# One early small read of x beside the first loads, and the last 256 output columns as one tile, two copies and one store

## The chip, the cores and the metric

The kernel runs on one core of a Trainium2 chip. The metric is the device time in microseconds (us) of that core, taken as the median of several runs; less is better. The profile of one run has a "span" that is about 1.8 us shorter than the time of the same run. Each kernel has one profile, of one execution.

## The reference

```python
def reference(x, gamma, w_qkv, eps):        # x: 8 x 1024 x 768, w_qkv: 768 x 2304, float32
    rms = np.sqrt(np.mean(x ** 2, axis=-1, keepdims=True) + eps)
    x_norm = x / rms * gamma
    return np.matmul(x_norm, w_qkv).astype(np.float32)
```

It is a matrix product of 8192 rows with 768 x 2304 weights, with a scale per row. The kernel folds gamma into the weights (converted to bf16) and applies 1/rms when it copies the product out of PSUM.

## The kernel before

Rows are worked in 64 tiles of 128. For the first six (the head) a fixed plan says in which order small loads, transposes and matmuls come; the rest is a steady loop. Loads and stores are issued by the sync engine (SP), gamma by ScalarE.

```python
LOADS = [  # order of issue on SP: "w" is a chunk of weights, "x" a tile of 128 rows (384 KB)
    (-9.00, "w", 0), (-8.99, "x", 0), (-8.98, "x", 1), (-8.97, "x", 2), (-8.96, "w", 1),
    (-8.95, "w", 2), (-8.94, "w", 3), (-8.93, "x", 3), (-8.92, "w", 4), ...
]
PARTS = [(0, 1024), (1024, 1024), (2048, N - 2048)]        # column ranges of an output row; the last is 256 wide
...
    g6 = singles.tile([KO, P], f32)
    nc.scalar.dma_start(out=g6, in_=gamma.rearrange("(ko p) -> ko p", p=P))
    eps_sb = singles.tile([P, 1], f32)
    nc.vector.memset(eps_sb, float(eps))
    tbl = singles.tile([P, 1], f32)
    nc.scalar.activation(out=tbl, in_=eps_sb, func=AF.Sqrt)      # loads ScalarE's table early
...
    def width(t, n0):                                            # columns of one PSUM tile
        return P if t == MT - 1 and n0 >= N - 2 * P else min(NT, N - n0)

    def evac(t, n0, eng):                                        # PSUM -> SBUF, times 1/rms
        nl = width(t, n0)
        ...
        if eng == "DVE":
            nc.vector.tensor_scalar(out=o, in0=pm[:, :nl], scalar1=RS[t], scalar2=None, op0=mult)
        else:
            nc.scalar.activation(out=o, in_=pm[:, :nl], func=AF.Copy, scale=RS[t], bias=0.0)
...
    def evac_at(time, t, n0, eng, gap):
        at(time, evac, t, n0, eng)
        h = part(n0)
        nl = width(t, n0)
        left[t, h] = left.get((t, h), PARTS[h][1]) - nl
        if t >= MT - 2:                                          # last two tiles: a store per copy
            at(time + gap - 0.5, store, t, h, n0, nl)
        elif left[t, h] == 0:
            at(time + gap, store, t, h, *PARTS[h])
...
        for n0 in [*range(0, N, NT)] + [N - P] * (t == MT - 1):  # last tile: 4 x 512, 128, 128 columns
            at(now, mm, t, n0, range(KO))
            now += width(t, n0) * US
            flip ^= 1
            evac_at(now + 0.2, t, n0, "DVE" if flip else "ACT", gap=1.2)
```

So the very end of the kernel is: a 512-wide PSUM tile copied by VectorE and stored (256 KB), then two 128-wide PSUM tiles, one copied by ScalarE and one by VectorE, each with its own store of 64 KB.

Of the kernel before, what the change touches and what calls it, by code (L numbers as in the profile page):

```python
# [10 lines left out]
HEAD = 6  # L11
# [81 lines left out]
def kernel(  # L93
# [8 lines left out]
    nc = tc.nc  # L102
    f32 = mybir.dt.float32
    bf16 = mybir.dt.bfloat16
    AF = mybir.ActivationFunctionType
    mult = mybir.AluOpType.mult

    xf = x.flatten_outer_dims()
    of = out.flatten_outer_dims()
    M, K = xf.shape  # L110
    Kw, N = w_qkv.shape
    assert K == Kw
    P = 128
    KO = K // P
    MT = M // P
    NT = 512
# [6 lines left out]
    singles = ctx.enter_context(tc.tile_pool(name="singles", bufs=1))  # L123
# [11 lines left out]
    ones = nc.const_aps.tensor(1.0, [P, NT], bf16)  # L135
    g6 = singles.tile([KO, P], f32)
    nc.scalar.dma_start(out=g6, in_=gamma.rearrange("(ko p) -> ko p", p=P))
    eps_sb = singles.tile([P, 1], f32)
    nc.vector.memset(eps_sb, float(eps))

# [10 lines left out]
    X, XB, XT, RS, OUT, WF, PM, PT = {}, {}, {}, {}, {}, {}, {}, {}  # L151
# [71 lines left out]
    begun = {}  # L223

    def width(t, n0):

        return P if t == MT - 1 and n0 >= N - 2 * P else min(NT, N - n0)

    def mm(t, n0, kos):
        nl = width(t, n0)  # L230
        for ko in kos:
            if (t, n0) not in PM:
                PM[t, n0] = psum.tile([P, NT], f32, name="pm")
            b = begun[t, n0] = begun.get((t, n0), 0) + 1
            nc.tensor.matmul(out=PM[t, n0][:, :nl], lhsT=XT[t][:, ko, :], rhs=w_b[:, ko, n0:n0 + nl],  # L235
                             start=(b == 1), stop=(b == KO))

    def part(n0):
        return max(i for i, (p0, _) in enumerate(PARTS) if p0 <= n0)

    def evac(t, n0, eng):
        nl = width(t, n0)
        h = part(n0)
        if (t, h) not in OUT:
            OUT[t, h] = outp.tile([P, PARTS[h][1]], f32, name=f"ot{h}")
        o = OUT[t, h][:, n0 - PARTS[h][0]:n0 - PARTS[h][0] + nl]
        pm = PM[t, n0]
        if eng == "DVE":
            nc.vector.tensor_scalar(out=o, in0=pm[:, :nl], scalar1=RS[t], scalar2=None, op0=mult)  # L249
        else:  # L250
            nc.scalar.activation(out=o, in_=pm[:, :nl], func=AF.Copy, scale=RS[t], bias=0.0)  # L251

    def store(t, h, n0, nl):
        p0 = PARTS[h][0]
# [6 lines left out]
    def at(time, fn, *args):  # L261
        plan.append((time, len(plan), fn, args))
# [8 lines left out]
# [5 lines that stand above are left out]
        if t >= MT - 2:  # L276
# [3 lines that stand above are left out]
# [27 lines left out]
    for t in range(HEAD, MT):  # L307

        ahead = 6.0 if t < HEAD + 5 else 0.0
        if ("x", t) not in {q[1:] for q in LOADS}:  # L310
            at(now - 15 - ahead, load_x, t)
        at(now - 8.5 - ahead, cast, t)
        at(now - 7.5 - ahead, xbar, t)
        at(now - 5, stat, t)
        at(now - 3, recip, t)
        for n0 in [*range(0, N, NT)] + [N - P] * (t == MT - 1):
            at(now, mm, t, n0, range(KO))
            now += width(t, n0) * US
            flip ^= 1
            evac_at(now + 0.2, t, n0, "DVE" if flip else "ACT", gap=1.2)  # L320
# [38 lines left out]
```

## Time and profile before

| | before |
|---|---|
| time, median of 3 runs | 388.26 us (388.1 to 388.3) |
| time in the runs beside the changed kernel, 6 runs | 388.21 us (387.88 to 388.62) |
| time and span of the profiled run | 388.64 us, 386.857 us |
| first main matmul | 8.09 us |
| span end, counted from the start of the last 512-wide copy | 4.292 us |

The page and the two ends are shown in the prediction below. ScalarE's timeline at the start (start, duration, engine, line, operation): the issue of the gamma load, then the table load.

```profile
0.73 0.58 ACTq L137 DMA_DIRECT2D g<-in_gamma_dram  x1
1.35 1.28 ACT L142 ACT_TABLE_LOAD   x1 [1.35 <-PEq L340]
```

A stretch of the chain of work that ended last:

```profile
16.13 6.01 DMA x_t<-in_x_dram
...
22.75 6.20 DMA xT<-xb
28.95 0.05 issue
```

After the head, x is transposed by a DMA (xT<-xb). At 28.95 us the chain passes from such a DMA to TensorE.

### The profile page before, as it was taken

How to read it: one execution, taken by the hardware profiler on the slowest of the kernel's cores; microseconds unless marked ns; L12 is line 12 of the kernel's file. 1: busy time of each engine (PE TensorE's matmuls, PEld its weight loads, DVE VectorE, ACT ScalarE, POOL GpSimd, SP SyncE). 2: the span in 40 equal slices, each digit the busy share in tenths (PEclk: the TensorE clock that was granted, in tenths of full speed). 3: DMA queues.
4: the chain of work that ended last, by engine and by line, in shares of the span. 5: the costliest groups of instructions: out<-in, count | busy, mean ns of one | idle time of the engine just before them, and what ended most of it. 6: DMA issues, size and time to landing. Idle time of an engine off the chain costs nothing.

```text
span 386.9 us, 5470 instructions
## 1 busy us (share of the span) xinstructions
PE 379.9 (98%) x1927; PEld 192.2 (50%) x1965; DVE 153.4 (40%) x307; ACT 181.6 (47%) x365; POOL 6.5 (2%) x14
## 2 busy tenths in 40 slices
PE   8999999999999999999999999999999999999996
PEld 4444655454554554554554554554554554554553
DVE  2744534434333344333344333343333343333332
ACT  4752644453544443544444444544444534434532
POOL 0130000000000000000000000000000000000000
PEclk9999999999999999999999999999999999999999
DMA  8999999999999999999999999999999999999985
GB/s 291 390 281 402 398 318 363 344 338 283 351 297 308 303 295 321 293 300 322 305 289 313 285 318 312 293 309 275 326 311 297 304 317 305 304 306 289 292 264 186
DMA packets 89719, 119.91 MB, mean 310 GB/s; under 512 B 52438, under 2 KB 61532, under 8 KB 89692
## 3 DMA queue, kind: packets, MB, share of 16 engines
q1 hardware_dynamic: 89680, 119.56, 101.2%
q8 instruction: 15, 0.25, 0.3%
q14 instruction: 12, 0.10, 0.1%
q10 hardware_dynamic: 12, 0.00, 0.0%
HBM read 32.25 MB, written 75.50 MB: 279 GB/s over the span
## 4 chain that ended last, share of the span: by engine, by line
PE 89%; DMA 8%; issue 1%; DVE 1%; ACT 1%; SPq 0%
PE pm L235 89%; DMA x_t<-in_x_dram 3%; DMA w_f<-in_w_qkv_dram 2%; DMA xT<-xb 2%; DMA out_dram<-ot 1%; ACT ot L251 1%; DVE ot L249 0%; DVE xb L174 0%; SPq L160 0%; SPq L155 0%; SPq L255 0%; ACT w_b L168 0%
## 5 line engine op out<-in xcount | busy, mean ns | idle before, releaser
L235 PE MATMUL pm<-w_b,xT 128*128 128x512 bf16 (+1 forms) x1888 | 372.1, 357 | 2.1
L235 PEld LDWEIGHTS <-xT 128*128 128x128 bf16 x1926 | 187.9, 98 | 185.5 <-DMA xT<-xb 0.5
L249 DVE TENSOR_SCALAR ot<-pm,rstd 128x512 f32<-128x512 f32 (+1 forms) x161 | 111.5, 695 | 206.1 <-PE pm L235 201.7
L251 ACT ACTIVATE ot<-pm,rstd 128x512 f32<-128x512 f32 (+2 forms) x160 | 102.7, 643 | 191.7 <-PE pm L235 151.0
L185 ACT ACTIVATE sq<-x_t 128x768 bf16<-128x768 f32 x64 | 53.4, 834 | 3.0 <-DMA x_t<-in_x_dram 3.0
L174 DVE CAST xb<-x_t 128x768 bf16<-128x768 f32 x61 | 33.2, 545 | 13.6 <-DMA x_t<-in_x_dram 13.5
L187 ACT ACTIVATE rms<-ssq,eps_sb 128x1 f32<-128x1 f32 x64 | 18.8, 294 | 2.1
L185 ACT ACTIVATION_READ_ACCUMULATOR sq<-x_t 128x1 f32 x64 | 12.2, 191 | 0.0
L166 DVE TENSOR_SCALAR w_b<-w_f,g_sb 128x512 bf16<-128x512 f32 (+1 forms) x16 | 7.7, 499 | 5.9 <-DMA w_f<-in_w_qkv_dram 5.9
L192 DVE RECIPROCAL rstd<-rms 128x1 f32<-128x1 f32 x64 | 9.8, 153 | 0.0
L170 POOL TENSOR_SCALAR w_b<-w_f,g_sb 128x512 bf16<-128x512 f32 (+1 forms) x8 | 5.8, 735 | 23.5 <-DMA w_f<-in_w_qkv_dram 23.5
L284 PE MATMUL pm<-const-bfloat16-1.0 128*128 128x512 bf16 (+1 forms) x14 | 5.4, 539 | 0.8 <-PEq L340 0.8
L168 ACT ACTIVATE w_b<-w_f,g_sb 128x512 bf16<-128x512 f32 (+1 forms) x6 | 3.6, 612 | 2.7 <-DMA w_f<-in_w_qkv_dram 2.7
L212 PE MATMUL pm<-ident_f,x_t 128*128 128x128 f32 x18 | 2.8, 300 | 0.3 <-DMA x_t<-in_x_dram 0.3
L212 PEld LDWEIGHTS pm<-ident_f,x_t 128*128 128x128 f32 x18 | 2.4, 160 | 1.3 <-DMA x_t<-in_x_dram 0.9
L284 PEld LDWEIGHTS <-const-bfloat16-1.0 128*128 128x128 bf16 x14 | 1.5, 126 | 2.7 <-issue 2.7
L176 ACT CAST xT<-pm 128x256 bf16<-128x256 f32 (+1 forms) x5 | 2.3, 458 | 0.9 <-PE pm L212 0.7
L142 ACT ACT_TABLE_LOAD x1 | 1.3, 1283 | 1.4 <-PEq L340 1.4
L174 DVE CAST xT<-pm 128x512 bf16<-128x512 f32 x1 | 0.7, 691 | 1.4 <-PE pm L212 1.4
L267 DVE COPY g_sb<-pm 128x6 f32<-128x6 f32 x1 | 0.2, 164 | 1.9 <-PE pm L266 1.9
L266 PEld LDWEIGHTS pm<-ident_f,g 6*128 6x128 f32 x1 | 0.2, 177 | 1.0 <-issue 1.0
L174 DVE COPY xT<-pm 128x768 bf16<-128x768 bf16 x1 | 0.6, 557 | 0.0
(12 smaller groups left out, 2.5 us busy)
## 6 DMA issues: line engine op xcount, KB each, us to landing
out_dram<-ot SPq DMA_DIRECT2D x124, 512.0 KB, 3.9
x_t<-in_x_dram SPq DMA_DIRECT2D x64, 384.0 KB, 4.2
out_dram<-ot SPq DMA_DIRECT2D x63, 128.0 KB, 3.2
w_f<-in_w_qkv_dram SPq DMA_DIRECT2D x10, 512.0 KB, 7.4
out_dram<-ot SPq DMA_DIRECT2D x8, 256.0 KB, 2.0
w_f<-in_w_qkv_dram SPq DMA_DIRECT2D x4, 256.0 KB, 6.6
xT<-xb SPq DMA_TRANSPOSE x60, 4.3
w_f<-in_w_qkv_dram SPq DMA_DIRECT2D x2, 384.0 KB, 6.1
```

What stands on the lines that cost most here:

```text
L166: nc.vector.tensor_scalar(out=o, in0=i, scalar1=g, scalar2=None, op0=mult)
L168: nc.scalar.activation(out=o, in_=i, func=AF.Copy, scale=g, bias=0.0)
L170: nc.gpsimd.tensor_scalar(out=o, in0=i, scalar1=g, scalar2=1.0, op0=mult, op1=mult)
L174: nc.vector.tensor_copy(out=out, in_=in_)
L185: nc.scalar.activation(out=sq, in_=X[t], func=AF.Square, accum_out=ssq)
L187: nc.scalar.activation(out=rms, in_=ssq, func=AF.Sqrt, scale=inv_k, bias=eps_sb)
L192: nc.vector.reciprocal(out=r, in_=RS[t])
L212: nc.tensor.transpose(out=PT[t, h][:, ko - k0, :], in_=X[t][:, ko * P:(ko + 1) * P], identity=ident_f)
L235: nc.tensor.matmul(out=PM[t, n0][:, :nl], lhsT=XT[t][:, ko, :], rhs=w_b[:, ko, n0:n0 + nl], start=(b == 1), stop=(b == KO))
L249: nc.vector.tensor_scalar(out=o, in0=pm[:, :nl], scalar1=RS[t], scalar2=None, op0=mult)
L251: nc.scalar.activation(out=o, in_=pm[:, :nl], func=AF.Copy, scale=RS[t], bias=0.0)
L284: nc.tensor.matmul(out=wps[:, :nl], lhsT=ones[:, :P], rhs=ones[:, :nl], start=True, stop=True)
```

## The change

The first part adds a small DMA on ScalarE: 16 floats of every sixteenth row of the head's 768 rows, 48 pieces of 64 bytes, into a tile that nobody uses. What it can be meant for is the loads of x that come after it. The second part ends the last row tile with one 256-column PSUM tile: VectorE copies its first half, ScalarE its second, and one 128 KB store takes the place of two of 64 KB.

```diff
     nc.scalar.dma_start(out=g6, in_=gamma.rearrange("(ko p) -> ko p", p=P))
+    touch = singles.tile([HEAD * P // 16, 16], f32)
+    nc.scalar.dma_start(out=touch, in_=xf[:HEAD * P].rearrange("(r s) k -> r s k", s=16)[:, 0, :16])
...
     def width(t, n0):
-        return P if t == MT - 1 and n0 >= N - 2 * P else min(NT, N - n0)
+        return min(NT, N - n0)
...
-        if eng == "DVE":
-            nc.vector.tensor_scalar(out=o, in0=pm[:, :nl], scalar1=RS[t], scalar2=None, op0=mult)
-        else:
-            nc.scalar.activation(out=o, in_=pm[:, :nl], func=AF.Copy, scale=RS[t], bias=0.0)
+        both = t == MT - 1 and n0 + nl == N
+        d = nl if eng == "DVE" and not both else P if both else 0
+        if d:
+            nc.vector.tensor_scalar(out=o[:, :d], in0=pm[:, :d], scalar1=RS[t], scalar2=None, op0=mult)
+        if d < nl:
+            nc.scalar.activation(out=o[:, d:], in_=pm[:, d:nl], func=AF.Copy, scale=RS[t], bias=0.0)
...
-        for n0 in [*range(0, N, NT)] + [N - P] * (t == MT - 1):
+        for n0 in range(0, N, NT):
```

## The prediction

> **What bounds the kernel now.** I read the page first, then the chain of work that ended last, then the timelines of the two ends, because the change touches nothing in between.
>
> ```profile
> span 386.9 us, 5470 instructions
> PE 379.9 (98%) x1927; PEld 192.2 (50%) x1965; DVE 153.4 (40%) x307; ACT 181.6 (47%) x365; POOL 6.5 (2%) x14
> ...
> L235 PE MATMUL pm<-w_b,xT 128*128 128x512 bf16 (+1 forms) x1888 | 372.1, 357 | 2.1
> ```
>
> TensorE is the bound: its main matmuls are 372.1 us busy in a span of 386.9 us, and it idled only 2.1 us ahead of them. The span is 1.4 us shorter than the time of 388.26 us; I take that offset as constant. So the change can only win in the two places where TensorE isn't streaming: the start, before about 8.1 us, and the tail, after the last matmul at about 383.2 us.
>
> The start, from the chain in order of time, TensorE's timeline, and the table by windows (its columns: stretch, length, busy us of each engine, clock, DMA share, GB/s):
>
> ```profile
> 1.75 5.58 DMA x_t<-in_x_dram
> 7.33 0.02 issue
> 7.35 7.38 DMA w_f<-in_w_qkv_dram
> ...
> 28.99 6.00 PE pm L235 x27
> ```
>
> ```profile
> 5.91 1.14 PE L212 MATMUL pm<-ident_f,x_t 128*128 128x128 f32 x6
> 7.38 0.88 PE L212 MATMUL pm<-ident_f,x_t 128*128 128x128 f32 x6 [0.32 <-DMA x_t<-in_x_dram]
> 8.09 0.59 PE L235 MATMUL pm<-w_b,xT 128*128 128x512 bf16 x2
> ```
>
> ```profile
> 1.00:2.00 1.00, 1.00 (x3) 0.29 (x2) 0.23 (x1) 0.65 (x1) 0.29 (x1) 1.00 0.34 25
> 2.00:3.00 1.00, 1.00 (x3) 0.15 (x1) 0.00 (x0) 0.84 (x2) 0.00 (x0) 1.00 0.64 197
> 3.00:4.00 1.00, 0.86 (x4) 0.46 (x4) 0.16 (x1) 0.00 (x0) 0.00 (x0) 1.00 1.04 389
> 4.00:5.00 1.00, 1.00 (x3) 0.30 (x2) 0.38 (x1) 0.00 (x0) 0.00 (x0) 1.00 1.08 405
> 5.00:6.00 1.00, 1.00 (x4) 0.43 (x3) 0.51 (x2) 0.50 (x1) 0.00 (x0) 1.00 1.05 366
> 6.00:7.00 1.00, 1.00 (x7) 0.82 (x5) 0.12 (x1) 0.73 (x3) 0.00 (x0) 1.00 0.95 367
> ```
>
> The reader is to see three things. The chain leaves through the load of the second tile of x (issued 1.75, landed 7.33 us). TensorE, which must transpose that tile next, idles 0.32 us for it. And the DMA engines are busy in 1-3 us while moving little (share 0.34 at 25 GB/s, 0.64 at 197 GB/s), and again move a little less in 5-7 us (366 against 405 GB/s): some early packets are slow. The first x tile landed at 5.48 us (ScalarE starts on it at 5.50), so the second came 1.85 us later, while 384 KB at the 405 GB/s seen beside it take 0.97 us. About 0.88 us was lost there (estimate from these figures).
>
> The tail, from three timelines of short windows and the DMA view:
>
> ```profile
> 382.56 1.02 DVE L249 TENSOR_SCALAR ot<-pm,rstd 128x512 f32<-128x512 f32 x2 [1.84 <-DMA out_dram<-ot]
> 382.90 0.37 ACT L251 ACTIVATE ot<-pm,rstd 128x128 f32<-128x128 f32 x1 [0.94 <-PE pm L235]
> ...
> 383.34 0.33 SPq L255 DMA_DIRECT2D out_dram<-ot  x1
> ...
> 384.24 0.40 SPq L255 DMA_DIRECT2D out_dram<-ot  x1
> ...
> out_dram<-ot SPq DMA_DIRECT2D x1, 64.0 KB, 1.6
> ```
>
> VectorE's row is two copies, 512 and 128 wide, done at 383.58; ScalarE's 128-wide copy is done at 383.27. Yet the last store goes out only at 384.24: the sync queue issues the previous two stores at 383.34 and 383.77, some 0.45 us apart. So issue, not copying, spaces the last three stores. The last lands 1.6 us after its issue, at 385.86, and 1.0 us of closing follows.
>
> **What the Trainium skill says.**
> - "PSUM — Partial Sum Buffer", section "PSUM bank collisions raise a hardware error": no two engines may touch the same bank and quadrant at once, "ScalarE-read with VectorE-read included". Before the change the two last copies overlap (382.90 to 383.27 beside 382.56 to 383.31), but out of different PSUM tiles, which agrees. After it they read one PSUM tile, and the built program indeed makes ScalarE's last copy wait for VectorE, where it waited for TensorE before. "At once" becomes one after the other.
> - "DMA: Bandwidth & Descriptors", section "Issuing engines are not separate DMA queues": a DMA from ScalarE runs on the same 16 engines and interleaves. So the touch competes with the loads. The small gamma load that ScalarE already issues does the same, on its own queue.
> - "TensorE: Matmul & The Clock Gate", section "Wait — 56ns, not 53.3ns?": start to start is N/2.4 GHz + about 2.5 ns, so 55.8 ns at 128 columns and 109.2 ns at 256. In the trace, the last twelve 128-wide matmuls start 55 to 56 ns apart, which agrees.
> I found no passage on a slow first read of an address, which is what the touch seems to be meant for.
>
> **The change part by part.**
> 1. *One more DMA on ScalarE's queue.* 48 rows of 64 B. The gamma issue took 0.58 us (0.73 to 1.32), so I expect about 0.6 us for this one, and the table load (1.28 us, now at 1.35) moves to about 1.95. It ends at 3.2 us, the warming activation near 3.5; ScalarE's first work is at 5.50. Cost on the path: 0.
> 2. *Completion semaphores.* The program rotates eight of them over the DMAs. The touch shifts each by one, but each load still waits for the one eight before it. New are two: the third single-chunk load of w waits for gamma (issued at 3.64, gamma's packets were through by 2.8), and the fourth x tile waits for the touch (issued at 4.14). I expect the touch landed by 4; even at 5 that tile's data only flow at 8.6, behind a full queue. Cost: 0.
> 3. *What the touch does to x.* Gamma's packets began about 1 us after the start of its issue, so the touch's begin near 2.4 us, while x's first data flow from 3.6. It is early enough. If the slow packets in x's second tile are first-touch stalls, that tile lands up to 0.88 us sooner; TensorE gains its 0.32 us of idling, or up to 0.48 us once the pipeline's drain is counted (0.59 us lie between the last transpose's start of the one tile and the first of the next, where 0.11 us is usual). The 512 KB loads behind it also move up, so I let the gain survive. But I doubt the cause: the later chunks of w and the fourth to sixth tiles of x, also never read before, show one packet above 150 ns in the trace between 9 and 20 us, where before 7 us there are some thirty. The stalls look tied to the first microseconds, not to addresses. And a touch that stalls does so on the same 16 engines.
>    Gain: 0 to 0.5 us, 0.15 expected.
> 4. *The last 256 columns.* TensorE: twelve matmuls at 55.8 ns (0.67 us) become six at 109.2 ns (0.66 us): -0.01 us. VectorE: its 128 columns still end at 383.58, after the 512-wide copy that ends at 383.31. ScalarE: starts some 0.05 us later, takes 0.37 us as before: done at 384.00. Store: issued at 384.04 in place of 384.24. Against this, one 128 KB store where two of 64 KB went, with its first half no longer ahead: the last packets add about 0.15 us (8 rows of 1 KB per engine at 46 ns, 0.37 us, against 8 of 512 B at 27 ns, 0.22 us). Gain: 0.20 - 0.15 + 0.01, about 0.05 us.
>
> Sum: 0.15 + 0.05 = 0.2 us of 388.26. I lean a little further to 388.0, since the 0.5 us of part 3 is all on the path if it comes.
>
> **The rivals.**
> - *The touch wins in full.* For it: the slow packets and the chain through x's second tile. Against: the clean later loads. It would make 387.7 with the tail.
> - *The touch hurts.* Its 48 reads take the stalls themselves, three per engine, ahead of w's first chunk and x's first tile. For it: the shared engines, and w's first packets being the slowest of all. Against: x's first tile isn't urgent, since TensorE runs warming matmuls until 5.91 us while it landed at 5.48: 0.43 us of slack. A stall of 1 us would cost about 0.5: 388.7.
> - *The tail gets worse.* ScalarE behind VectorE, then one larger store. If the 0.05 us of semaphore delay is 0.1 and the store lands in 1.9 us instead of 1.6, the tail loses 0.15 us: about 388.4 without help from the touch.
> - *All hidden:* 388.2.
>
> **Range and chances.** Best case 0.5 + 0.15, worst 0.5 + 0.15 the other way; runs of the kernel before spread over 0.2 us. An interval from 387.3 to 388.6 holds most of these, lopsided towards faster because the touch was aimed at a wait that is on the chain. 2% is 7.8 us, more than the whole start before the first main matmul, so either verdict but "same" needs something outside this working.
>
> **What would show it.** Part 1: a second issue row of ScalarE near 1.35 and the table load near 1.95. Part 3: the idle time of 0.32 us before the second tile's transposes, its landing at 7.33, and the first main matmul at 8.09; if they stand, the touch does nothing, and if 8.09 becomes 7.6, it won. Part 4: ScalarE's last copy after VectorE's, at about 383.64 relative to an unmoved TensorE, one store at 384.04, landing 1.75 us later. The prediction would be wrong if TensorE's stream broke later on, say because earlier loads bring earlier stores that collide with the transposing DMAs around 29 us, or if the head's order of landings changed so that a weight conversion came late.

## The result, and the profile after

The changed kernel took 388.48 us (387.99 to 389.42, six runs), the kernel before 388.21 us (387.88 to 388.62, six runs). The ratio is 1.0008 with a 95% interval of 0.9994 to 1.0021: the same.

The page of the changed kernel is almost the same as before, with six matmuls fewer:

```profile
span 386.9 us, 5457 instructions
...
PE 379.8 (98%) x1921; PEld 191.4 (49%) x1959; DVE 153.2 (40%) x307; ACT 181.5 (47%) x365; POOL 6.6 (2%) x14
```

The two spans even agree to the third decimal, 386.857 us. That is a coincidence of three terms, which the next views show. First the start: ScalarE's timeline, with the touch and the table load.

```profile
1.35 0.33 ACTq L140 DMA_DIRECT2D touch<-in_x_dram  x1
1.71 1.28 ACT L145 ACT_TABLE_LOAD   x1 [1.71 <-PEq L345]
...
5.74 0.84 ACT L188 ACTIVATE sq<-x_t 128x768 bf16<-128x768 f32 x1 [2.53 <-DMA x_t<-in_x_dram]
```

The touch is issued in 0.33 us and the table load moves by 0.36 us, long before ScalarE has anything to do at 5.74 us. The list of DMA issues gives the touch's size and its time from issue to landing:

```profile
touch<-in_x_dram ACTq DMA_DIRECT2D x1, 3.0 KB, 3.6
```

It landed at 4.91 us. Its packets were served from 3.68 to 4.40 us, and x's own first packets from 3.71 us: the touch isn't ahead of x but beside it. TensorE's timeline and the table by windows (stretch, length, busy us of each engine, clock, DMA share, GB/s) answer to those of the prediction:

```profile
5.76 0.88 PE L215 MATMUL pm<-ident_f,x_t 128*128 128x128 f32 x6
7.13 0.88 PE L215 MATMUL pm<-ident_f,x_t 128*128 128x128 f32 x6 [0.50 <-DMA x_t<-in_x_dram]
7.85 0.59 PE L237 MATMUL pm<-w_b,xT 128*128 128x512 bf16 x2
```

```profile
1.00:2.00 1.00, 1.00 (x3) 0.29 (x2) 0.23 (x1) 0.29 (x1) 0.29 (x1) 1.00 0.31 30
2.00:3.00 1.00, 1.00 (x4) 0.15 (x2) 0.00 (x0) 0.99 (x1) 0.00 (x0) 1.00 0.78 199
...
5.00:6.00 1.00, 1.00 (x5) 0.27 (x4) 0.73 (x2) 0.27 (x1) 0.00 (x0) 1.00 1.07 350
6.00:7.00 1.00, 0.64 (x6) 0.40 (x4) 0.55 (x1) 0.97 (x4) 0.00 (x0) 1.00 0.91 363
```

The wait for the second tile of x hasn't gone; it is 0.50 us where it was 0.32. The busy engines that move little in 2-3 us are there too (0.78 at 199 GB/s). Still the first main matmul comes 0.24 us earlier in this profile, because the second tile landed at 7.09 us and not at 7.33.

Most of that lead was lost by 24 us. In the chain of work that ended last, the passage from a transposing DMA to TensorE has moved from 28.95 to 24.18 us:

```profile
2.69 6.07 DMA w_f<-in_w_qkv_dram
8.76 0.02 issue
8.77 7.63 DMA w_f<-in_w_qkv_dram
16.40 7.78 DMA xT<-xb
24.18 0.05 issue
24.22 10.75 PE pm L237 x49
```

TensorE's timeline has the wait itself (some matmul records are missing around it, so its length is rough):

```profile
24.22 0.60 PE L237 MATMUL pm<-w_b,xT 128*128 128x512 bf16 x2 [0.27 <-DMA xT<-xb]
```

In the run before, the same transpose had landed at 22.92 us, in time. A second wait for such a transpose follows at 73.9 us; here the weight loads (PEld) show it:

```profile
73.94 0.55 PEld L237 LDWEIGHTS <-xT 128*128 128x128 bf16 x4 [0.32 <-DMA xT<-xb]
```

It moved the stream by 0.21 us. From there on the changed kernel ran 0.19 us behind the kernel before, and the tail gave just this back. The tail, from timelines of short windows (VectorE, ScalarE, then the two last stores on SP's queue):

```profile
382.76 1.01 DVE L254 TENSOR_SCALAR ot<-pm,rstd 128x512 f32<-128x512 f32 x2 [1.84 <-PE pm L237]
383.80 0.37 ACT L256 ACTIVATE ot<-pm,rstd 128x128 f32<-128x128 f32 x1 [1.65 <-DVE ot L254]
...
383.54 0.33 SPq L260 DMA_DIRECT2D out_dram<-ot  x1
...
384.19 0.33 SPq L260 DMA_DIRECT2D out_dram<-ot  x1
```

ScalarE's last copy now follows VectorE's ("<-DVE ot"), as the page "PSUM — Partial Sum Buffer" of the Trainium skill, quoted in the prediction, made likely. The store leaves at once after it.

To compare tails whose starts differ, I count from S, the start of VectorE's last 512-wide copy (382.565 us before, 382.756 after). These come from single records of the trace:

| us after S | before | changed |
|---|---|---|
| VectorE's 128 columns done | 1.02 | 1.01 |
| ScalarE's 128 columns done | 0.70 | 1.41 |
| 256 KB store issued | 0.777 | 0.779 |
| its packets, first start to last end | 1.610 to 2.448 | 1.608 to 2.456 |
| next store(s) issued | 1.202 and 1.678 | 1.439 |
| last packet ends | 2.937 | 2.815 |
| last store landed | 3.292 | 3.164 |
| polls of other completion semaphores after that | 3 | 2 |
| span ends | 4.292 | 4.101 |

So the tail is 0.19 us shorter: 0.13 from the landing and 0.06 from one poll less. The medians don't show it, which the experiments have to explain: something else of the same size moves.

### The profile page after: what moved, and what is told of

It is laid out like the page before. It is cut to its first block, busy times and chain, and to the rows that moved or that the text cites. A ratio compares the mean times of both kernels' runs of the same rounds, so it can differ in the third digit from the quotient of the medians.

```text
span 386.9 us, 5457 instructions
## 1 busy us (share of the span) xinstructions
PE 379.8 (98%) x1921; PEld 191.4 (49%) x1959; DVE 153.2 (40%) x307; ACT 181.5 (47%) x365; POOL 6.6 (2%) x14
## 4 chain that ended last, share of the span: by engine, by line
PE 92%; DMA 6%; issue 1%; SPq 0%; DVE 0%; ACT 0%; DVEq 0%
PE pm L237 92%; DMA w_f<-in_w_qkv_dram 4%; DMA xT<-xb 2%; SPq L158 0%; DVE ot L254 0%; SPq L163 0%; ACT ot L256 0%; DVEq L359 0%
```

## The experiments

All runs in one table. "First matmul" is the first main matmul in the profiled run, "x tile 2" the landing of x's second tile, "slow packets" the number of packets over 0.2 us in the loads of x's first three tiles (of 128 packets each), "tail" the time from S to the end of the span. The kernel before stands with the runs of the same chip, since chips differ: touch_only to half_store_on_act ran on one, x_before_w and the two reads on a second, change_again to four_quarters on a third. Which chip the profile of the kernel before is from isn't recorded, so starts are best compared within a group.

| kernel | median us (range), runs | before on that chip | ratio, 95% | first matmul | x tile 2 | slow packets | tail |
|---|---|---|---|---|---|---|---|
| before | 388.21 (387.88-388.62), 6 | | | 8.09 | 7.33 | 1, 6, 5 | 4.292 |
| changed | 388.48 (387.99-389.42), 6 | 388.21 | 1.0008, 0.9994-1.0021 | 7.85 | 7.09 | 1, 9, 1 | 4.101 |
| touch_only | 388.56 (388.23-388.68), 5 | 388.28 | 1.0005, 0.9992-1.0018 | 7.46 | 6.71 | 0, 1, 1 | 4.374 |
| tail_only | 388.07 (387.95-388.11), 5 | 388.28 | 0.9994, 0.9981-1.0006 | 7.69 | 6.93 | 0, 3, 0 | 4.034 |
| two_banks_one_store | 388.27 (388.04-388.44), 5 | 388.28 | 0.9998, 0.9986-1.0011 | 7.43 | 6.67 | 0, 0, 4 | 4.093 |
| half_store_on_act | 388.63 (388.38-389.11), 5 | 388.28 | 1.0009, 0.9995-1.0023 | 7.57 | 6.81 | 0, 3, 0 | 4.319 |
| x_before_w | 392.06 (390.08-392.73), 6 | 388.63 | 1.0078, 1.0052-1.0104 | 9.52 | 4.85 | 19, 9, 5 | 4.290 |
| read_same_first | 393.28, 1 | 388.63 | | 11.54 | 9.85 | 0, 2, 0 | |
| read_other_first | 393.41, 1 | 388.63 | | 11.59 | 9.90 | 3, 4, 0 | |
| change_again | 388.31 (388.11-388.73), 5 | 388.55 | 0.9999, 0.9985-1.0013 | 7.77 | 6.80 | 0, 1, 1 | 4.097 |
| touch_16_rows | 388.49 (388.19-388.72), 5 | 388.55 | 0.9999, 0.9987-1.0012 | 7.70 | 6.94 | 0, 1, 0 | 4.381 |
| touch_every_row | 388.85 (388.46-389.15), 5 | 388.55 | 1.0008, 0.9996-1.0021 | 8.13 | 7.38 | 0, 0, 0 | 4.397 |
| four_quarters | 387.93 (387.77-388.10), 5 | 388.55 | 0.9985, 0.9972-0.9997 | 7.53 | 6.77 | 1, 3, 1 | see there |

### Each half of the change alone

touch_only is the kernel before with the two lines of the touch. tail_only is the changed kernel without them.

```diff
 # touch_only, against before
+    touch = singles.tile([HEAD * P // 16, 16], f32)
+    nc.scalar.dma_start(out=touch, in_=xf[:HEAD * P].rearrange("(r s) k -> r s k", s=16)[:, 0, :16])
 # tail_only, against changed
-    touch = singles.tile([HEAD * P // 16, 16], f32)
-    nc.scalar.dma_start(out=touch, in_=xf[:HEAD * P].rearrange("(r s) k -> r s k", s=16)[:, 0, :16])
```

> Only the touch is added to the kernel before. Theory A (the touch does nothing for x, because the slow early packets belong to the first microseconds and not to addresses): the second x tile lands at 7.0 to 7.5 us, TensorE still idles 0.3 us or more before its transposes, the first main matmul starts at 7.7 to 8.2 us, and the median is within 0.4 us of the kernel before. Theory B (the touch opens x's addresses): the second tile lands near 6.5 us, the first main matmul starts by 7.6 us, and the median is 0.3 to 0.5 us lower. Theory C (the touch costs time): the median is 0.3 us or more higher.

> Only the new tail: one 256-wide PSUM tile, VectorE and ScalarE copy half each, one store. Counted from the start of VectorE's last 512-wide copy, the span ended 4.29 us later before and 4.10 us later with both parts of the change. Theory: the tail alone gives that 0.19 us, so again 4.05 to 4.15 us, ScalarE's copy again starting after VectorE's; median about 0.2 us below the kernel before, hardly to be told from the spread. Rival (the 0.19 us came from the touch or from chance): 4.25 us or more.

touch_only came out at 388.56 us and tail_only at 388.07 us, with 388.28 us for the kernel before on that chip. Both intervals include 1, but the tail goes the way that the trace says. tail_only's tail is 4.034 us, 0.26 less than before and just under the 4.05 to 4.15 expected: 0.13 from the landing and 0.13 from two polls fewer.

touch_only's start met the mark that was set for Theory B (first matmul by 7.6 us), though its median did not. More telling is the column of the first matmul. tail_only has no touch, and its second x tile landed at 6.93 us and its first matmul came at 7.69 us, both earlier than with the touch in the changed kernel. Two more kernels without a touch on touch_only's chip came at 7.43 and 7.57 us, around touch_only's 7.46. On the third chip four_quarters, without one, came at 7.53 us, before all three that had one. In these four kernels without a touch the second tile landed 0.96 to 0.98 us after the first: the 0.88 us that the prediction counted as lost are missing without any touch. So a quick start isn't the touch's doing. The profile of the kernel before had a late one, in a long execution (388.64 us); whether its chip had a part in that isn't known.

Nor did the touch remove the slow packets. Counting all loads that started before 7 us, the kernels without a touch had 28 to 32 packets over 0.2 us (before, tail_only, two_banks_one_store, half_store_on_act, four_quarters), those with one 20 to 31. In x's tiles alone they were a few fewer with the touch on the same chips (0 to 2 against 3 to 5); the starts show no gain from that.

touch_only also shows a cost that nobody had in mind. Its tail is 4.374 us, 0.08 longer than before, with the same copies and the same three stores. The last instructions of SP poll the completion semaphores one after the other. The program deals eight of them out in turn, and one more DMA at the start shifts the turn, so that the last store's semaphore is now polled first: four polls follow it where three did, some 0.06 us each. (The remaining 0.02 us are a later landing.)

### Is it the copies, the store's issue or its data that end the kernel?

two_banks_one_store keeps the two 128-wide PSUM tiles and their copies side by side, and replaces only the two stores by one. half_store_on_act keeps two stores, but ScalarE issues the first of them.

```diff
 # two_banks_one_store, in evac_at
+        if t == MT - 1 and h == 2:
+            if left[t, h] == 0:
+                at(time + gap - 0.5, store, t, h, *PARTS[h])
-        if t >= MT - 2:
+        elif t >= MT - 2:
             at(time + gap - 0.5, store, t, h, n0, nl)
 # half_store_on_act, in store
+        q = nc.scalar if t == MT - 1 and n0 == N - 2 * P else nc.sync
-        nc.sync.dma_start(out=..., in_=...)
+        q.dma_start(out=..., in_=...)
```

> The kernel before, with its two 128-wide PSUM tiles kept, but one 128 KB store of the last 256 columns. Theory (in the changed kernel ScalarE's copy waits for VectorE's because they read one PSUM tile, and that wait eats most of the saved issue): here ScalarE's copy is done before VectorE's, the store is issued at once when VectorE ends or the queue is free, about 1.2 us after the start of VectorE's last 512-wide copy, where the changed kernel took 1.44 us and the kernel before 1.68 us; the span ends 3.85 to 3.95 us after that start (before 4.29, changed 4.10); median 0.3 to 0.4 us below before. Rival (the store's own landing sets the end whatever the issue): 4.1 us or more.

> The kernel before, but ScalarE issues the store of its own last 128 columns, so the sync queue has one store less. Theory (the sync queue's issue spacing of 0.45 us is what delays the last store): the sync queue's last store moves from 1.68 to about 1.25 us after the start of VectorE's last 512-wide copy, and the span ends about 3.85 us after it, as with the single store out of two PSUM tiles. Rival (both issuers share what makes the descriptors, so the issue on ScalarE delays the sync queue's): no gain over 0.2 us, 4.1 us or more.

The tail of two_banks_one_store, from the same kind of timelines (S is 382.165 us here):

```profile
382.50 0.37 ACT L251 ACTIVATE ot<-pm,rstd 128x128 f32<-128x128 f32 x1 [0.94 <-PE pm L235]
...
382.94 0.33 SPq L255 DMA_DIRECT2D out_dram<-ot  x1
...
383.38 0.37 SPq L255 DMA_DIRECT2D out_dram<-ot  x1
```

Its last store was issued 1.216 us after S, 0.22 us earlier than in the changed kernel. It gained nothing by that: its first packet came 2.279 us after S (2.296 in the changed kernel) and its last ended at 2.813 (2.815). The reason is in the table of the tail above: the DMA engines are still writing the 128 rows of 2 KB of the 256 KB store ahead, at a median of 85 ns a packet, until about 2.45 us after S. The Trainium skill says as much in "DMA: Bandwidth & Descriptors", section "Queues, rings and completion order": "On each SDMA engine descriptors are consumed in ring order". The trace agrees: the first small store was issued at 1.202 us in the kernel before, at 1.216 here and at 1.439 in the changed kernel, and its data start to flow at one time, 2.28 to 2.30 us. The theory (a span end 3.85 to 3.95 us after S) failed: it was 4.093.

half_store_on_act freed SP's last issue in the same way:

```profile
383.49 0.40 ACTq L256 DMA_DIRECT2D out_dram<-ot  x1
...
383.96 0.38 SPq L256 DMA_DIRECT2D out_dram<-ot  x1
```

SP's last store goes out 1.203 us after S (1.678 before) and lands 3.320 us after S (3.292 before); the tail is 4.319 against 4.292 us. ScalarE's small packets went between those of the big store from 1.77 us on, and the big store's last ended at 2.616 us and not at 2.448. This is what the section "Issuing engines are not separate DMA queues", quoted in the prediction, says of two issuers, and the run agrees. So issue wasn't the main limit, but it had a part. In the kernel before, the DMA engines were partly idle between the two small stores. The table by windows shows it, for 2.5 to 2.7 us after S, before and then changed (the last two figures are the engines' busy share and GB/s):

```profile
385.06:385.26 0.20, 0.00 (x0) 0.00 (x0) 0.00 (x0) 0.00 (x0) 0.00 (x0) 1.00 0.77 223
```

```profile
385.26:385.46 0.20, 0.00 (x0) 0.00 (x0) 0.00 (x0) 0.00 (x0) 0.00 (x0) 1.00 0.94 318
```

The last store, issued at 1.678 us, could not flow before about 2.51 us if it needs the 0.83 us from issue to first packet that the 256 KB store took (an estimate). In half_store_on_act, with that issue at 1.203, the last packet ended at 2.886 us, 0.05 sooner than before. It landed no sooner all the same: 0.43 us passed from last packet to landing, where 0.36 passed before, and why isn't shown.

The last packet of the one store ends 0.12 us sooner than before. About 0.05 us of that is this idle stretch. The rest fits the form of the rows: packets of 1 KB took a median of 47 ns, those of 512 B 27 ns each and twice as many, which for 8 and 16 packets a DMA engine is 0.38 against 0.43 us (an estimate). The one store gains this with or without the shared PSUM tile.

### Is it the first read of an address that is slow?

The touch can only help if x's early packets are slow because their addresses had not been read. Both kernels below read three tiles into unused memory ahead of x's own loads. One reads x's first three tiles, the other three far away. If addresses matter, x's own loads are faster in the first only.

```diff
-    (-9.00, "w", 0), (-8.99, "x", 0),
+    (-9.00, "w", 0), (-8.997, "d", 0), (-8.996, "d", 1), (-8.995, "d", 2), (-8.99, "x", 0),
+    def load_d(n):
+        d = singles.tile([P, K], f32, name=f"d{n}")
+        t = 0 + n                     # read_other_first: 40 + n
+        nc.sync.dma_start(out=d, in_=xf[t * P:(t + 1) * P, :])
```

> Between the first chunk of w and the first x tile, the first three x tiles are read once in full into unused tiles, so every address of theirs has been read when the real loads follow. In the kernel before, 12 of the 384 packets of these three tiles took over 200 ns (usual 121), in the changed kernel about as many. Address theory: the unused reads show the dozen slow packets, the real reads none. Time theory (the first microseconds are slow whatever is read): the same, since the real reads start near 6.7 us. So this run alone does not decide; the next does. Time: about 3 us more than before for the 1.18 MB, less what is hidden.

> As the last one, but the unused reads are of three other x tiles (the 41st to 43rd), so the first three tiles' addresses are still new when their real loads follow. Address theory: the real reads show a dozen packets over 200 ns, as in the kernel before, and land later than in the run that read the same tiles first. Time theory: the real reads show none or two, and both runs land within 0.3 us of each other. Time: as the other run under the time theory; up to 0.9 us more under the address theory.

These are single looks at a clock of 0.99, state unknown, and of course slower by the time of three loads; only the head is read. TensorE's transposes of x in read_same_first, then in read_other_first:

```profile
8.93 2.82 PE L217 MATMUL pm<-ident_f,x_t 128*128 128x128 f32 x12 [3.71 <-DMA x_t<-in_x_dram]
```

```profile
8.97 2.82 PE L217 MATMUL pm<-ident_f,x_t 128*128 128x128 f32 x12 [4.03 <-DMA x_t<-in_x_dram]
```

The real tiles landed at 8.88, 9.85 and 10.85 us where the same addresses had just been read, and at 8.93, 9.90 and 10.89 us where they hadn't. The 0.05 us between them was there before x's own loads began: the last unused tile had landed at 7.91 and 7.96 us. From there the three real tiles took 2.94 us in one and 2.93 in the other, so a previous read was worth nothing here. The slow packets were in both cases mostly in the reads that came early (1, 9, 3 and 3, 8, 4 of 128 in the unused tiles); in those that followed there were 2 and 7. This speaks against the theory that the touch warms addresses, in one look each, and for reads as large as the tiles themselves.

### What if x comes first?

The next question was how much an earlier start is worth, and whether its lead survives. x_before_w loads x's first two tiles ahead of the first weights.

```diff
-    (-9.00, "w", 0), (-8.99, "x", 0), (-8.98, "x", 1), (-8.97, "x", 2),
+    (-8.975, "w", 0), (-8.99, "x", 0), (-8.98, "x", 1), (-8.97, "x", 2),
```

> The kernel before, with the first two x tiles loaded ahead of the first chunk of w: no byte added or taken. It makes the early x tiles come sooner without any touch, to ask what an earlier start is worth at the end. Expected: the second x tile lands near 6 us in place of 7.33, TensorE's wait for it vanishes, the first main matmul starts 0.2 to 0.5 us sooner (it then waits for w). Theory (an earlier start is taken back by TensorE's waits for the transposing DMAs near 24 and 29 us, as the changed kernel's trace suggests, where it led by 0.24 us at 8 us and by 0.02 us at 35 us): at 35 us TensorE is within 0.1 us of the kernel before and the median within 0.3 us. Rival (a gain at the start is kept): the median is lower by as much as the first main matmul is earlier.

As a way to start earlier it failed: 392.06 us. x's tiles landed at 3.91 and 4.85 us, but VectorE's copy of the first transposed tile stands in the program behind the conversion of the weights, and these now landed at 7.88 us. VectorE's timeline, then TensorE's:

```profile
7.98 0.88 DVE L166 TENSOR_SCALAR w_b<-w_f,g_sb 128x512 bf16<-128x512 f32 x2 [4.51 <-DMA w_f<-in_w_qkv_dram]
8.78 0.68 DVE L174 CAST xT<-pm 128x512 bf16<-128x512 f32 x1
```

```profile
9.52 0.99 PE L235 MATMUL pm<-w_b,xT 128*128 128x512 bf16 x2 [2.08 <-DVE xT L174]
```

It was useful all the same. I had thought that the waits for transposes at 24 to 29 us level out any difference of the start. They don't. The table shows when each kernel's copies out of PSUM start, against the same copy in the profile of before (plus is later, us):

| kernel | near 14.5 us | 29 us | 69 us | 77 us | 373 us |
|---|---|---|---|---|---|
| changed | -0.23 | -0.05 | -0.02 | +0.19 | +0.19 |
| touch_only | -0.56 | -0.54 | -0.50 | -0.50 | -0.50 |
| tail_only | -0.42 | -0.38 | -0.35 | -0.35 | -0.35 |
| two_banks_one_store | -0.69 | -0.65 | -0.62 | -0.40 | -0.40 |
| half_store_on_act | -0.54 | -0.51 | -0.51 | +0.19 | +0.19 |
| x_before_w | +2.77 | +2.65 | +2.80 | +2.80 | +2.80 |
| change_again | -0.56 | -0.34 | -0.32 | -0.32 | -0.32 |
| touch_16_rows | -0.43 | -0.41 | -0.40 | -0.40 | -0.40 |
| touch_every_row | +0.03 | +0.02 | +0.09 | +0.09 | +0.10 |
| four_quarters | -0.48 | -0.44 | -0.40 | -0.40 | -0.40 |

A lag or a lead at the start is kept to the end, unless TensorE happens to meet a late transpose near 24 us (changed, change_again) or near 74 us (changed, two_banks_one_store, half_store_on_act). From 77 us on nothing moves in any kernel. The late transposes near 74 us come with and without the touch. Those near 24 us came only in the two changed kernels, and not in touch_only, which is the same program up to the last row tile; so the touch doesn't always bring them, and whether it has a part isn't shown. The one at 73.95 us moved half_store_on_act by 0.70 us, more than either half of the change is worth; the trace puts 0.53 us of it down to the wait:

```profile
73.95 1.25 PE L235 MATMUL pm<-w_b,xT 128*128 128x512 bf16 x4 [0.53 <-DMA xT<-xb]
```

x_before_w also says something of the slow packets: now that x was read first, x's first tile had 19 of them. The weights' first chunk, read from 4.07 us on in this kernel, had 24 as well. So being read early goes with being slow whichever tensor it is, but it isn't only the very first DMA. Nor is it only the first microseconds: between 9 and 20 us this kernel had 24 load packets over 0.15 us where the kernel before had one. What makes these packets slow stays open.

### The touch smaller and larger, and the change again

touch_16_rows reads 64 B of each of the first 16 rows only; touch_every_row reads 64 B of every row of the head, 768 pieces. change_again is the changed kernel, unedited, on the chip of these runs.

```diff
 # touch_16_rows, against before
+    touch = singles.tile([16, 16], f32)
+    nc.scalar.dma_start(out=touch, in_=xf[:16, :16])
 # touch_every_row, against before
+    touch = singles.tile([P, HEAD, 16], f32)
+    nc.scalar.dma_start(out=touch, in_=xf[:HEAD * P].rearrange("(t p) k -> p t k", p=P)[:, :, :16])
```

> The changed kernel once more, on the same chip as the next three. So far it was 0.27 us above the kernel before, while its tail alone was 0.21 us below and its touch alone 0.28 us above. If the parts add up: within 0.2 us of before, and the last end of the span 4.1 us after the start of VectorE's last 512-wide copy, as before. If the touch harms: again 0.2 us or more above. The profile should again show either a wait for the transposing DMA near 74 us or none; I expect the lag at the end to be the first main matmul's lag plus these waits, whatever the medians do.

> The kernel before plus a touch of only 16 rows (one 64 B packet for each DMA engine). It has the touch's place in the rotation of the completion semaphores and its issue on ScalarE, but none of its spread over addresses. If the touch harms through the rotation: the closing polls after the last landing take 4 steps of about 0.06 us (before 3), and the median is as with the 48-row touch, 0.1 to 0.3 us above before. If it harms through its packets: within 0.1 us of before.

> The kernel before plus a touch of all 768 rows of the first six x tiles, 768 packets of 64 B, 48 for each DMA engine; at the 11 ns that such a packet took in the changed kernel's trace, 0.5 us of each engine. If the touch opened addresses, this one opens them all and the second x tile lands by 6.7 us in spite of it. If the packets only cost: the second x tile lands 0.3 to 0.6 us later than the 6.7 to 7.3 us seen so far, the first main matmul starts at 7.9 us or later, and the median is 0.4 us or more above before.

change_again came out at 388.31 us with 388.55 us before, ratio 0.9999: where the first comparison leaned to slower by 0.27 us in the medians, this one leans to faster by 0.24 us. touch_16_rows had the same ratio. With every row touched, x's loads showed no slow packet at all, and yet its second tile landed at 7.38 us, last of all kernels with x in the usual place (by 0.05 us). TensorE's timeline of touch_every_row:

```profile
7.42 0.88 PE L215 MATMUL pm<-ident_f,x_t 128*128 128x128 f32 x6 [0.34 <-DMA x_t<-in_x_dram]
8.13 0.59 PE L238 MATMUL pm<-w_b,xT 128*128 128x512 bf16 x2
```

Whatever keeps x's packets quick there, the small packets probably take the time themselves: 768 of 11 ns over 16 engines are 0.53 us (an estimate). All three touches without the new tail have a tail of 4.37 to 4.40 us, four polls at the end each.

### A version from what was learned

If the 256 KB store's data are the limit at the end, that store has to leave sooner. four_quarters has no touch. It splits the last 512 columns into two 256-wide PSUM tiles, so that VectorE copies the first while TensorE works on the second and ScalarE copies that; one 256 KB store follows. Then two 128-wide PSUM tiles, copied side by side, and one 128 KB store.

```diff
     def width(t, n0):
-        return P if t == MT - 1 and n0 >= N - 2 * P else min(NT, N - n0)
+        if t == MT - 1 and n0 >= N - 6 * P:
+            return P if n0 >= N - 2 * P else 2 * P
+        return min(NT, N - n0)
...
+        if t == MT - 1 and n0 >= 1536:
+            if n0 == 1792:
+                at(time + gap - 0.5, store, t, h, 1536, 512)
+            if n0 == 2176:
+                at(time + gap - 0.5, store, t, h, *PARTS[h])
-        if t >= MT - 2:
+        elif t >= MT - 2:
             at(time + gap - 0.5, store, t, h, n0, nl)
...
-        for n0 in [*range(0, N, NT)] + [N - P] * (t == MT - 1):
+        for n0 in range(0, N, NT) if t < MT - 1 else (0, 512, 1024, 1536, 1792, 2048, 2176):
```

> No touch. The tail as the last runs suggest it: the last 512-wide block is computed in two 256-wide PSUM tiles, copied by VectorE and ScalarE, and stored at once; the last 256 columns in two 128-wide PSUM tiles, copied by both, and stored at once. Theory (in the tail the last store's data wait for the 256 KB store ahead of it to drain, 0.84 us, so that store must go out sooner): the 256 KB store is issued some 0.3 us sooner relative to the last matmul, and the span ends about 3.6 us after the last matmul's start, where before it was 3.88 us, with the changed tail 3.7 to 3.76 us, with two PSUM tiles and one store 3.68 us. Median 0.2 to 0.4 us below before. Rival (the drain of the last store alone sets it): no better than 3.68 us.

The tail of four_quarters, VectorE and ScalarE in order of time, then SP's two last stores:

```profile
381.52 0.48 DVE L251 TENSOR_SCALAR ot<-pm,rstd 128x256 f32<-128x256 f32 x1 [1.20 <-PE pm L237]
382.18 0.47 ACT L253 ACTIVATE ot<-pm,rstd 128x256 f32<-128x256 f32 x1 [0.62 <-PE pm L237]
382.51 0.35 DVE L251 TENSOR_SCALAR ot<-pm,rstd 128x128 f32<-128x128 f32 x1 [0.51 <-PE pm L237]
382.85 0.37 ACT L253 ACTIVATE ot<-pm,rstd 128x128 f32<-128x128 f32 x1 [0.20 <-PE pm L237]
...
382.68 0.33 SPq L257 DMA_DIRECT2D out_dram<-ot  x1
...
383.24 0.33 SPq L257 DMA_DIRECT2D out_dram<-ot  x1
```

There is no 512-wide copy to count from, so count from the start of the last matmul, which is 128 wide here as in the kernel before (382.589 and 382.977 us). The 256 KB store leaves 0.086 us after it, where it left 0.365 us after it before: 0.279 us sooner. With the 0.19 us that the one store and the poll are worth, 0.47 us are to be expected; the span ends 3.393 us after that matmul's start and not 3.880, which is 0.487 us. About 3.6 us had been expected. The time was 387.93 us (387.77 to 388.10), with 388.55 us for the kernel before (388.13 to 389.58, whose upper runs widen the difference), ratio 0.9985, 0.9972 to 0.9997. It is the only version whose interval leaves out 1 on the fast side, and its median is below those of both kernels. Still it is far inside 2%.

## Why the prediction was right or wrong

Range held: 388.48 us lies in 387.3 to 388.6, and "same" was what it expected. But the lean of 0.26 us towards faster did not come, and the terms of the sum were off. The range could hardly miss: runs of the unchanged kernel alone filled 387.88 to 388.62.

- **The bound.** Right. Only start and tail can matter, with the addition that a few waits for transposes at 24 and 74 us can still move the stream by 0.2 to 0.7 us. The prediction named the danger at the end ("collide with the transposing DMAs around 29 us") but gave it no term. It also set the span of the profiled run against the median of other runs: that run took 388.64 us, so the offset was 1.8 us and not 1.4, and the execution it read was a long one.
- **Part 1, the issue.** Cost nothing, as predicted. It was 0.33 us, not 0.6, and the table load came at 1.71 us and not 1.95.
- **Part 2, the semaphores.** Right in its cost at the loads, half right in who waits. The third single-chunk load of w had gamma's semaphore, as predicted. The fourth x tile waited for the first weights and not for the touch, and was issued at 4.77 us (4.14 before). The touch's semaphore went to the next load of weights, but the touch had landed (4.91 us) before that load's turn at 5.18 us (4.73 before). Neither delay cost anything, because both loads then stand behind others in the DMA engines: that x tile's data flow at 8.7 us in any case. What the step overlooked is the other end of the rotation: it decides how many semaphores are still to be polled after the last store. Alone, the touch made the tail 0.08 us longer in that way.
- **Part 3, the touch on x.** This is the step that failed. It allowed 0 to 0.5 us and counted 0.15. The doubt in it was right as to addresses: reading the very addresses first gained nothing. As to time ("tied to the first microseconds") it is less sure, since x_before_w had slow packets at 18 us too. The sign that was named for a win, a first matmul at 7.6 us, is none, since kernels without a touch reach it. It was also wrong on the time: the touch's packets came 2.3 us after its issue, not 1, thus not ahead of x. The 0.32 us of idling that it hoped for was read from one profile; the first main matmul came anywhere from 7.43 to 8.09 us in the kernels without the touch and from 7.46 to 8.13 us in those with one (x_before_w and the two kernels with extra reads left out).
- **Part 4, the tail.** The new order, ScalarE after VectorE, was right; so were the matmuls (the 256-wide ones start 109 ns apart in both traces) and the landing, 1.725 us after the issue where 1.75 was predicted. The store went out 1.439 us after S; the 384.04 predicted were 1.475 after S. The gain was mis-sized: 0.19 us measured, 0.05 predicted. In the prediction's own terms, the issue came 0.24 us sooner (0.20 predicted), issue to landing grew by 0.11 us (0.15 charged), and one poll fewer gave 0.06 us, which was not counted. The reading behind it, "issue, not copying, spaces the last three stores", is true of the issues, but it sets the end only in small part. Issuing the one store another 0.22 us sooner changed nothing, since its data wait for the 256 KB store ahead.
- **The sum.** 0.2 us of gain expected, 0.19 us of shorter tail found, and a time that doesn't show it: the start and the waits for transposes vary by as much and more. That the two figures agree is luck, for three quarters of the expected gain were the touch's. The "spread over 0.2 us" that the range rested on came from three runs; six runs of the same kernel spread over 0.7 us, and nine on another chip over 1.4 us.
- **The rivals.** "The touch wins in full" is refuted. "All hidden" is nearest for the touch. "The tail gets worse" is refuted by the trace. "The touch hurts" holds for the 0.07 to 0.1 us of a longer tail; whether it costs more than that is not settled: touch_only was 0.28 us above the kernel before in the medians, touch_16_rows 0.06 below, and all their intervals include 1.

## What to carry to other kernels

Before crediting an early wait in one profile to a cause, look at the same place in a few profiles with an unchanged start: here it moved by 0.66 us among them, and by 0.26 us among three on one chip. At the end of a kernel, follow the data and not only the issue: here a small last store started when the large one ahead had drained, so sending the large one sooner gained most, and one store of longer rows gained a little over two. And when a test reads "the same", the trace can still say something of which half did what.

## What the Trainium skill lacked or had wrong

- "DMA: Bandwidth & Descriptors", section "Latency and other measured facts", gives about 600 ns to a first byte on this path. Here the first packet of the 256 KB store in the quiet tail came 0.83 us after the start of its issue (0.50 after its end), and that of the touch, beside the first loads, 2.3 us after. The page doesn't say from which moment it counts.
- No page that I found tells of slow packets in the first microseconds: up to 1.06 us for one packet of the weights' first chunk before and 1.53 us in x_before_w, where 84 ns is usual for 2 KB, and whichever tensor is read early.
- No page that I found tells of the polls of completion semaphores at the end, some 0.06 us each (3.348, 3.412, 3.474 us after S in the kernel before), nor that one more DMA at the start, or one store fewer at the end, changes how many of them come after the last landing (2 to 4 here, once 1).
- "Queues, rings and completion order" has the ring order but no number for what it does to a small store behind a large one: data at 2.28 to 2.30 us after S for issues at 1.202 to 1.439 us.
